# Rotary partners in two tiles: attention for four heads of four key heads at once

## The chip, the cores and the metric

The kernel runs on one core of a Trainium2 chip. The metric is device time in microseconds (us) of one execution of the whole program. Engines are TensorE (PE in the profile, with PEld for its weight loads), VectorE (DVE), ScalarE (ACT), GpSimd (POOL) and SyncE (SP, which here only issues transfers).

## The reference, cut to what matters

The reference is one inference step of a small decoder with two layers on 1024 prompt tokens and eight decode tokens, width 2048. Layer A is a pooling mixer with a gate. After it, keys and values for four key heads of 64 are projected once and shared. Layer B is attention over a window of 128 keys with 32 query heads, eight to a key head, with a sink per head, a gate and an output projection. The first 16 of a head's 64 dimensions are rotated by position ("partial rotary"): dimension i below 8 is the partner of dimension i + 8.

```python
x1, x2, rest = xf[..., :half], xf[..., half:ROT_DIM], xf[..., ROT_DIM:]
out = jnp.concatenate([x1 * cos - x2 * sin, x2 * cos + x1 * sin, rest], axis=-1)
...
s = jnp.einsum('...qkgd,...skd->...kgqs', q, k) * (HEAD_DIM ** -0.5)
p = jnp.exp(s - m);  p = p / (jnp.sum(p, axis=-1, keepdims=True) + jnp.exp(sink - m))
o = jnp.einsum('...kgqs,...skd->...qkgd', p, v);  y = (o * jax.nn.silu(gate)) @ w_out
```

## The kernel before, in words

The prompt is worked in two halves ("chunks"): chunk 0 has 512 tokens, chunk 1 has 512 and the eight decode tokens, 520 columns. Activations lie transposed, channels in partitions and tokens in columns. All large products are made in three passes of split operands: a high part, written by ScalarE (`cast_to`, L488), and a low part, written by VectorE (`prep_to`, L503). Most are made by a Strassen-like scheme of seven half-size products a pair of output tiles (`seven`, L582, products at L658 to L660). Two phases are "plain" (`unit`, L672, products at L686 to L688), and while they run, the sums of weight blocks that the later products need are made by VectorE and stored (`plain_pair`, L293; `first_pair`, L346).

The list `PHASES` sets the order. The attention phases are `bi`: chunk 0, head pairs 0 to 3, plain; chunk 0, pairs 4 to 7, by seven products; chunk 1, pairs 0 to 7, by seven products. After them come the output projections (`bo`). In a plain `bi` phase a unit makes one tile of 128 channels (two heads) by 512 tokens. It has 48 products in four steps of 12. With seven products a pair of tiles takes seven steps of 24 products.

The order of the small work is written by hand against this counter of steps, `self.i`. `at(n, go)` puts work n steps ahead; `product(n, rank, go)` puts PE work at the end of a step, ordered by rank; `posts` are done at the beginning of the next step. `in_order` then fixes the order of the source on PE, VectorE and ScalarE, so a late instruction holds everything behind it on its engine. Loads are issued on SP's queue in program order, a few entries of the weight stream ahead (`ahead`, `load_to`), and each waits until its buffer is free. Buffers are 53 slots of two times 520 columns (`Mem`); a new tile takes the slot that was released longest ago, whole or half.

Attention before the change handles one tile t of 128 query channels at a time: two heads of 64 rows, which belong to two key heads. The order of a head's dimensions is permuted so that the rotary partner of row r is row r + 32 or r - 32. So the rotary step (`q_done`, L1719; `k_done` for keys) copies the tile with neighbouring groups of 32 rows exchanged, by four transfers on SP's queue (`partner`, L1611, issued at L1616), and some steps later (`lag`) multiplies tile and copy by tables of cosine and sine (`rope`, L1624) and adds them (L1731).

`attend` (L1745) then has, for one tile t and all four blocks of 128 tokens: the scores (`score`, L1760), products of a 64-row, 64-column part of PE with 192 keys, into the four PSUM banks of `S`; `select` and `largest` (L1778, L1782, L1786), which put together 8 x 128 scores a row and take the maximum; exponential and sums; `turn` (L1814), eight transposes into the first half of `S`; `keep` (L1823 on ScalarE, L1824 on VectorE), two copies of the transposed weights; the second products (`values`, L1848), in two parts with a GpSimd flag between them (L1856); and `gate` (L1876), which multiplies by the gate and stores. Each has its step: scores at `at`, transposes `s1` steps later, second products `s2` steps after those. So the second products of an earlier tile and the scores of a later one fall on the same step: first part, scores, second part. `gate_done` (L1911) prepares the gate. `t_ops` (L820) makes and stores four differences and sums of a tile, the operands of later seven-product phases.

The next phase's inputs are loaded from `x_begin` on (`x_load`, L759) and split (L769, L778), as slots are free (`x_tick`). The eight decode tokens have their own attention (`dec_keys`, `decode`), for two key heads at a time: once in the middle of the last attention phase and once in the output phase after it, at the steps of `DEC_AT`.

## Time and profile before

| | |
|---|---|
| median of three runs | 2356.75 us (2353.7 to 2358.1) |
| profiled execution, its own time | 2356.38 us |
| span of that execution, first to last instruction | 2354.6 us |
| granted TensorE clock, mean | 0.996 |
| TensorE busy | 2297.3 us, 98% |
| VectorE, ScalarE, GpSimd busy | 82%, 57%, 9% |
| transfers | 665.18 MB, mean 283 GB/s |

A row of a list of groups has the line, engine and operation, then output<-inputs by the program's names, then shape and count; after the bar busy us and mean ns of one; after the next bar the idle time of that engine just before and what ended it. A row of the timeline begins with the start and the duration in us; in brackets is the idle time before it and what ended it. A row of the list of waits reads: who, for whom, us in total, times, longest. In a row of windows each engine has busy us and (in brackets) its instructions, and behind them stand the granted clock, the transfer engines' busy share and GB/s. One matmul of 32-bit operands appears as two instructions, its two passes.

The page's forty slices show how evenly TensorE is filled:

```
PE   8999999999999999999999899999999999999997
DVE  8787998776878878978987788887777768888887
DMA  8668789989889989999786766688777768799785
```

### The profile page before, as it was taken

The numbers are of one execution on the slowest core, as the hardware profiler recorded it, in microseconds if no ns is written. First come the engines' busy times: TensorE is split into PE (matmuls) and PEld (weight loads), VectorE is DVE, ScalarE is ACT, GpSimd is POOL, SyncE is SP. The second block draws the span as 40 slices with busy tenths as digits, with TensorE's granted clock in tenths as the row PEclk, the third lists the DMA queues.
The fourth block names the chain that finished last, engine by engine and source line by source line (L and its number), as shares of the span: only waits on it lengthen the run. The fifth ranks groups of instructions, "written<-read, shape, count | busy, mean of one in ns | idle before, by whom it ended". The sixth has DMA issues, their size and how long they took to land. (4 is left out here: it accounts for less than half of the span.)

```text
span 2354.6 us, 49710 instructions
## 1 busy us (share of the span) xinstructions
PE 2297.3 (98%) x19960; PEld 2200.9 (93%) x19960; DVE 1925.9 (82%) x2421; ACT 1343.1 (57%) x2429; POOL 205.5 (9%) x411
## 2 busy tenths in 40 slices
PE   8999999999999999999999899999999999999997
PEld 6899999999999999998788799999999999999997
DVE  8787998776878878978987788887777768888887
ACT  4444446544546547554465566685666678546556
POOL 0111110001000000000111111100000000000000
PEclk9999999999999999999999999999999999999999
DMA  8668789989889989999786766688777768799785
GB/s 293 211 246 303 271 299 346 332 292 319 289 289 339 327 280 333 328 388 327 272 310 220 248 219 239 224 310 270 237 249 245 230 201 305 239 342 372 260 300 199
DMA packets 250919, 665.18 MB, mean 283 GB/s; under 512 B 25632, under 2 KB 106432, under 8 KB 250688
## 3 DMA queue, kind: packets, MB, share of 16 engines
q1 hardware_dynamic: 205216, 496.94, 63.0%
q0 software_dynamic: 45472, 165.07, 18.1%
q8 instruction: 156, 2.56, 0.4%
q14 instruction: 75, 0.61, 0.1%
HBM read 466.81 MB, written 185.59 MB: 277 GB/s over the span
## 5 line engine op out<-in xcount | busy, mean ns | idle before, releaser
L658 PE MATMUL pD<-m,m 128*128 128x260 f32 (+1 forms) x4752 | 1346.0, 283 | 8.1 <-ACT pD L599 4.4
L660 PE MATMUL pD<-m,m 128*128 128x260 f32 (+1 forms) x4752 | 1339.1, 282 | 4.4 <-DVE m L503 4.4
L659 PE MATMUL pD<-m,m 128*128 128x260 f32 (+1 forms) x4752 | 1338.8, 282 | 0.0
L658 PEld LDWEIGHTS pD<-m,m 128*128 128x128 f32 x4752 | 894.5, 188 | 13.7 <-ACT pD L599 5.5
L660 PEld LDWEIGHTS pD<-m,m 128*128 128x128 f32 x4752 | 895.2, 188 | 5.5 <-DVE m L503 5.5
L503 DVE TENSOR_TENSOR m<-m,m 128x1024 fp32r<-128x1024 f32 x674 | 814.5, 1219 | 100.1 <-ACT m L488 60.6
L659 PEld LDWEIGHTS pD<-m,m 128*128 128x128 f32 x4752 | 894.9, 188 | 0.5
L488 ACT CAST m<-m 128x1024 fp32r<-128x1024 f32 x674 | 702.7, 1049 | 324.7 <-DVE m L346 85.1
L686 PE MATMUL pD<-m,m 128*128 128x512 f32 x448 | 179.7, 401 | 8.0 <-ACT m L769 8.0
L687 PE MATMUL pD<-m,m 128*128 128x512 f32 x448 | 177.9, 397 | 1.0 <-DVE m L778 1.0
L688 PE MATMUL pD<-m,m 128*128 128x512 f32 x448 | 177.5, 396 | 0.0
L778 DVE TENSOR_TENSOR m<-m,m 128x1024 fp32r<-128x1024 f32 (+1 forms) x120 | 147.0, 1226 | 6.4 <-ACT m L769 4.7
L769 ACT CAST m<-m 128x1024 fp32r<-128x1024 f32 (+1 forms) x120 | 125.9, 1053 | 17.7 <-PE pD L687 5.2
L631 ACT COPY m<-pD 128x260 f32<-128x260 f32 (+1 forms) x83 | 31.1, 375 | 179.2 <-PE pD L660 179.1
L346 DVE TENSOR_TENSOR m<-m,m 128x1024 f32<-128x1024 f32 x88 | 107.6, 1222 | 12.7 <-DMA m<-in_wib 6.3
L686 PEld LDWEIGHTS pD<-m,m 128*128 128x128 f32 x448 | 85.1, 190 | 28.1 <-ACT m L769 8.0
L687 PEld LDWEIGHTS pD<-m,m 128*128 128x128 f32 x448 | 85.0, 190 | 21.1 <-DVE m L778 2.1
L688 PEld LDWEIGHTS pD<-m,m 128*128 128x128 f32 x448 | 85.0, 190 | 19.7
L1797 ACT ACTIVATE m<-m,sm 128x128 f32<-128x128 f32 x256 | 99.4, 393 | 0.0
L619 DVE TENSOR_TENSOR m<-pD,m 128x260 f32<-128x260 f32 (+1 forms) x86 | 36.5, 424 | 74.4 <-PE pD L660 74.1
L1088 PE MATMUL pD<-m,m 128*128 128x260 f32 (+1 forms) x528 | 91.5, 323 | 0.0
L1088 PEld LDWEIGHTS pD<-m,m 128*128 128x128 f32 x528 | 79.5, 188 | 8.2
(249 smaller groups left out, 2180.9 us busy)
## 6 DMA issues: line engine op xcount, KB each, us to landing
m<-in_wia SPq DMA_DIRECT2D x124, 512.0 KB
m<-in_wib SPq DMA_DIRECT2D x120, 512.0 KB
swia<-m POOLq DMA_DIRECT2D x64, 512.0 KB, 4.8
m<-swia SPq DMA_DIRECT2D x64, 512.0 KB
m<-swoa SPq DMA_DIRECT2D x64, 512.0 KB
swib<-m POOLq DMA_DIRECT2D x64, 512.0 KB, 5.1
m<-swib SPq DMA_DIRECT2D x64, 512.0 KB
m<-swob SPq DMA_DIRECT2D x56, 512.0 KB
```

The source lines that it names most:

```text
L346: self.nc.vector.tensor_add(s[out].a[:, :1024], s[x].a[:, :1024], s[y].a[:, :1024])
L488: self.nc.scalar.copy(hi.r[:, :1024], self.stream[self.cast].src().a[:, :1024])
L503: self.nc.vector.tensor_sub(lo.r[:, :1024], s.src().a[:, :1024], hi.a[:, :1024])
L658: nc.tensor.matmul(ps[:, :TH], wh[:, s], h, start=new and k == 0, stop=False, skip_group_check=on)
L659: nc.tensor.matmul(ps[:, :TH], wh[:, s], l, start=False, stop=False, skip_group_check=on)
L660: nc.tensor.matmul(ps[:, :TH], wl[:, s], h, start=False, stop=k == 7, skip_group_check=on)
L686: nc.tensor.matmul(ps[:], wh[:, s], h, start=par == 0 and k == 0, stop=False)
L687: nc.tensor.matmul(ps[:], wh[:, s], l, start=False, stop=False)
L688: nc.tensor.matmul(ps[:], wl[:, s], h, start=False, stop=par == 1 and k == 7)
L769: self.nc.scalar.copy(h.r[:, :n], s.a[:, :n])
L778: self.nc.vector.tensor_sub(l.r[:, :n], s.a[:, :n], h.a[:, :n])
L1088: nc.tensor.matmul(ps[:, : cs.stop - cs.start], ws[:, s], d[:, cs], start=f0 and k == 0, stop=l0 and k == 3,)
```

## The change

The heads are reordered: head pair p now stands for four heads, one of each of the four key heads, in two tiles of 128 rows. Tile 0 holds 32 of the dimensions of all four, among them the first rotary half (rows 32g to 32g + 31 for key head g), tile 1 the other 32. Partners are therefore in the same partition of the two tiles, the partner transfers go, and the rotary step is four VectorE operations on the pair. The keys are laid out likewise. A score is then the sum of two products of 32 rows, accumulated in PSUM, and a step of attention takes four heads and half of the blocks (`hf`), where it took two heads and all blocks. Both tiles of a pair must be there before a score.

With it go other edits. In the plain phase the weights come pair after pair, units 0 and 1 of a pair make the queries and 2 and 3 the gates, and both halves of attention hang on one rotary step. Steps are shifted: the rotary step is issued one step after its tiles there, and with lag 2 in place of 3 in the seven-product phases; transposes and second products of the last three halves of the plain phase are one step apart; the gate of the plain phase goes to the next step's beginning; `x_begin` of the plain phase's end comes before the second unit of the last pair. The decode tokens of all four key heads are handled at once, in the output phase. `t_ops` makes two of its differences by one instruction everywhere it is called.

```diff
-DEC_AT = (0, 1, 6, 6, 7, 8, 9, 10, 13, 13), (11, 11, 12, 12, 13, 14, 15, 16, 17, 17)
+DEC_AT = 3, 3, 9, 9, 10, 11, 12, 12, 14, 14
...
-                        q, g = pr("wib", p), pr("wib", 8 + p)
-                        w += q[:2] + g[:2] + q[2:] + g[2:]
+                        w += pr("wib", p) + pr("wib", 8 + p)
...
-        nc.vector.tensor_sub(t[:, 1, :], E[:, a], E[:, b])
-        nc.vector.tensor_sub(t[:, 2, :], E[:, b], O[:, b])
+        E, O = v[:, 0], v[:, 1]
+        h = v.rearrange("p j (h n) -> p j h n", h=2)
+        nc.vector.tensor_sub(t[:, 1:3, :], h[:, 0], h[:, :, 1])
...
-    def partner(self, s, n, T):
-        t = self.mem.full()
-        for a in range(4):
-            b = a ^ 1
-            self.nc.sync.dma_start(t.a[32 * a : 32 * a + 32, : n * T], s.a[32 * b : 32 * b + 32, : n * T])
-        return t
-    def rope(self, s, t, n, T):
-        b2 = lambda x: x[:, None, :].to_broadcast([P, n, T])
-        for a, i in ((s, 0), (t, 1)):
-            v = a.v(n, T)
-            self.nc.vector.tensor_mul(v, v, b2(self.rtab[:, i, :T]))
+    def rope(self, s, T):
+        nc = self.nc
+        u = self.mem.full()
+        v, w = s.v(2, T), u.v(2, T)
+        sin = self.rtab[:, 1, :T]
+        nc.vector.scalar_tensor_tensor(w[:, 0], v[:, 1], -1.0, sin, op0=ALU.mult, op1=ALU.mult)
+        nc.vector.tensor_mul(w[:, 1], v[:, 0], sin)
+        nc.vector.tensor_mul(v, v, self.rtab[:, :1, :T].to_broadcast([P, 2, T]))
+        return u
...
-    def q_done(self, c, t0, s, n, lag):
+    def q_done(self, c, p, s, lag):
...
+        def turn():
+            u = self.rope(s, T)
+            nc.vector.tensor_add(s.a[:, : 2 * T], s.a[:, : 2 * T], u.a[:, : 2 * T])
+            u.free()
...
+        self.at(lag, turn)
...
-            for b in range(NB):
-                for u in (0, 64):
-                    for j in range(2):
-                        r = slice(64 * j, 64 * j + 64)
-                        nc.tensor.matmul(
-                            self.S[u : u + 64, j, b * 256 + u : b * 256 + u + 192],
-                            q[r, b * P + u : b * P + u + 64],
-                            self.kT[t // 8][r, b * P + u : b * P + u + 192], start=True, stop=True,
-                        )
+            for n in range(2):
+                b = 2 * hf + n
+                for i in range(2):
+                    q = s.a[:, i * T : i * T + TP]
+                    for u in (0, 64):
+                        for g in range(4):
+                            r = slice(32 * g, 32 * g + 32)
+                            nc.tensor.matmul(
+                                S4[u : u + 64, g, n * 256 + u : n * 256 + u + 192],
+                                q[r, b * P + u : b * P + u + 64],
+                                self.kT[i][r, b * P + u : b * P + u + 192], start=i == 0, stop=i == 1,
+                            )
...
             if self.i in self.scores:
                 self.product(0, 3, lambda: values(1))
-                self.at(1, gate)
+                if self.strassen:
+                    self.at(1, gate)
+                else:
+                    self.posts.append(gate)
...
-            for t in range(2 * ps[0], 2 * ps[-1] + 2):
...
-                n = t - 2 * ps[-1]
-                self.attend(c, t, 9, *{-1: (11, 1), 0: (13, 2), 1: (8, 2)}.get(n, (14, 2)), n == 0)
-                self.unit(q_done)
-                if t == 2 * ps[-1] - 1:
-                    self.x_begin(nxt)
-                self.last = t == 2 * ps[-1] + 1
-                self.unit(g_done)
+            for p in ps:
+                for hf in range(2):
+                    n = 2 * (p - ps[-1]) + hf
+                    self.attend(
+                        c, p, hf, 10 + 8 * hf, *{-1: (13, 1), 0: (13, 1), 1: (8, 1)}.get(n, (14, 2)), n in (-1, 0)
+                    )
+                box = {}
+                for n in range(4):
+                    def take(ps, n=n, p=p, box=box):
+                        if n % 2 == 0:
+                            box["s"] = self.mem.full()
+                        nc.scalar.copy(box["s"].a[:, n % 2 * T : (n % 2 + 1) * T], ps[:])
+                        if n == 1:
+                            self.q_done(c, p, box["s"], 1)
+                        elif n == 3:
+                            self.gate_done(c, p, box["s"])
+                    if p == ps[-1] and n == 1:
+                        self.x_begin(nxt)
+                    self.last = p == ps[-1] and n == 3
+                    self.unit(take)
...
-            if T > TP and p % 4 == 3:
-                self.at(2, lambda p=p: self.dec_keys(p // 4))
+            if T > TP and p == 7:
+                self.at(6, self.dec_keys)
...
-            self.pair(c, z0, z1, lambda t0=t0, box=box: self.q_done(c, t0, box["s"], 2, 3))
+            self.pair(c, z0, z1, lambda: self.q_done(c, p, box["s"], 2))
...
-                if T > TP and p % 4 == 3:
-                    self.decode(c, p // 4)
+                if T > TP and p == 7:
+                    self.decode(c)
...
-_HEADS = np.array([16 * pr + 8 * j + i for pr in range(2) for i in range(8) for j in range(2)])
+_HEADS = np.array([8 * g + p for p in range(8) for g in range(NKV)])
```

300 lines of the change are left out of this document (143 added, 157 removed).

## The prediction

> **What bounds the kernel now.** I read the page's first part, then the list of what TensorE (PE) waited for, then single waits in the timeline.
>
> ```profile
> span 2354.6 us, 49710 instructions
> PE 2297.3 (98%) x19960; PEld 2200.9 (93%) x19960; DVE 1925.9 (82%) x2421; ACT 1343.1 (57%) x2429; POOL 205.5 (9%) x411
> ```
>
> PE is busy for 98% of the span, so only two things move the end: PE's own work, and the 57 us in which it stands. Another engine matters where it ends one of those waits.
>
> ```profile
> PE pS L1760 <- DVE m L1731: 8.4, 8, 1.5
> PE pD L686 <- ACT m L769: 8.0, 1, 8.0
> PE pO L1848 <- ACT m L1823: 7.8, 1, 7.8
> PE pD L660 <- DVE m L503: 4.4, 5, 1.4
> ...
> PE pS L1760 <- DVE m L1731: 6.8, 6, 1.5
> ```
>
> Columns: us, times, longest. The change can reach two rows: the scores (L1760) waiting for the rotary add (L1731), 8.4 us, and one wait of 7.8 us of the attention's second product (L1848). The 8.0 us are the kernel's first load. The last row is the same view cut to 1345 to 2000 us, the part of the attention phases written with seven products: 6.8 of the 8.4 us lie there, 1.7 us in the first four head pairs of half 0 ("plain" below).
>
> **The rotary partners.** Each rotary step first moves partner rows with four transfers on SP's queue.
>
> ```profile
> L1616 SPq DMA_DIRECT2D m<-m x88: 512/588/2031, 1106.0 to 1957.9; - x88
> ...
>   DMA m<-m: 11.6, 6
> ...
> 1624.94 2.39 DVE L1624 TENSOR_TENSOR m<-m,m 128x1040 f32<-128x1040 f32 x2 [3.86 <-DMA m<-m]
> 1627.37 1.24 DVE L1731 TENSOR_TENSOR m<-m,m 128x1040 f32<-128x1040 f32 x1
> ```
>
> The second row is what VectorE (DVE) idled for ahead of the rotary products (L1624): 11.6 us for the partners. Removed are 88 transfers of 64 KB and 88 x 0.59 = 52 us of SP's time. SP is off PE's path, so that by itself is worth nothing; what counts is the score.
>
> In the seven-product parts the rotary work stays about as long: three operations of 1040 columns before, now two of 520 and two of 1040.
>
> ```profile
> L1624 DVE TENSOR_TENSOR m<-m,m 128x1040 f32<-128x1040 f32 x18 | 21.5, 1236 | 6.8 <-DMA m<-m 6.8
> L1624 DVE TENSOR_TENSOR m<-m,m 128x1024 f32<-128x1024 f32 x10 | 11.8, 1220 | 4.9 <-DMA m<-m 4.9
> L1624 DVE TENSOR_TENSOR m<-m,m 128x512 f32<-128x512 f32 x16 | 10.3, 684 | 0.0
> ```
>
> Before 3 x 1.24 = 3.7 us, after 2 x 0.69 + 2 x 1.24 = 3.9. But it is issued one step earlier (lag 2, not 3; a step there is 24 products of 0.12 us, 2.9 us) and waits for no transfer. The longest wait in this part is 1.5 us, so all six should go: **-6.8 us**, bounds 0 (VectorE late for another reason, such as the buffer of the new temporary) and -6.8.
>
> In the plain part one rotary step now serves two tiles at once, with the same lead as before: two operations of 512 and two of 1024 columns (2 x 0.68 + 2 x 1.22 = 3.8 us) in place of three of 512 (2.05). The first half's score waits for all of it.
>
> ```profile
> 1157.97 1.53 PE L1760 MATMUL pS<-m,m 64*64 64x192 f32 x32 [1.49 <-DVE m L1731]
> ...
> 1203.68 1.23 DVE L1824 TENSOR_TENSOR m<-pS,cst 128x1024 f32<-128x1024 f32 x1 [0.81 <-ACT m L1823]
> 1204.83 1.28 DVE L1624 TENSOR_TENSOR m<-m,m 128x512 f32<-128x512 f32 x2
> 1206.14 0.69 DVE L1731 TENSOR_TENSOR m<-m,m 128x512 f32<-128x512 f32 x1
> ...
> 1207.04 0.28 PE L1848 MATMUL pO<-m,m 64*64 64x128 f32 x2
> 1207.06 0.28 PE L1848 MATMUL pD<-m,m 64*64 64x128 f32 x2
> ...
> 1207.27 0.28 PE L1848 MATMUL pO<-m,m 64*64 64x128 f32 x2
> ...
> 1207.38 0.28 PE L1848 MATMUL pO<-m,m 64*64 64x128 f32 x2
> ...
> 1207.56 0.22 PE L1848 MATMUL pD<-m,m 64*64 64x64 f32 x2
> 1207.60 1.48 PE L1760 MATMUL pS<-m,m 64*64 64x192 f32 x32
> ```
>
> The add ends at 1206.83, 0.77 us before PE is ready. With 1.75 us more it is 1.0 us late. Half as many scores wait: three at 1.0 us, and the first, which waits 1.49 us today (1157.97), about the same; 4.5 less the 1.7 of today is **+2.8 us**. Bounds: -1.7 (VectorE uses the 0.81 us in which it idles ahead) and +4.5 (the first one also grows by 1.75).
>
> **The scores on PE.** A score has 32 products of 64 rows today (16, in two passes), in rounds of four array tiles: 1.48 us less the last one's 0.32, over seven rounds, is 0.16 us a round. The change has 64 products of 32 rows, each as long. Eight tiles at once make again eight rounds of 0.16 us; four at once make sixteen, +1.3 us a score. In the rows above a round of four starts within some 0.02 us (1207.04 and 1207.06, two each), so issue can fill eight tiles in 0.16 us. I take **0**, upper bound 32 x 1.3 = +42.
>
> Then the switch of tile shape. Today scores and second products are both 64x64, and most scores stand between two groups of second products. After the change they are 32x64 between 64x64.
>
> ```profile
> 1209.75 0.23 PE L1848 MATMUL pO<-m,m 64*64 64x64 f32 x2
> 1209.90 0.50 PE L686 MATMUL pD<-m,m 128*128 128x512 f32 x1
> ...
> 1206.88 0.33 PE L1848 MATMUL pO<-m,m 64*64 64x128 f32 x2
> ...
> 1971.46 0.23 PE L1848 MATMUL pD<-m,m 64*64 64x64 f32 x2
> 1971.51 1.48 PE L1760 MATMUL pS<-m,m 64*64 64x192 f32 x32
> ```
>
> Within one shape the next group starts 0.04 us after the last (1207.56 to 1207.60). To another shape it is 0.15 us (1209.75 to 1209.90), 0.11 more, and the first round after a switch takes 0.16 us (1206.88 to 1207.04) where a later one takes 0.11 (1207.27 to 1207.38), 0.05 more: 0.16 us a switch. 24 of the 32 scores stand so, the first at 1207.60, the last at 1971.51; two new switches each are 48 x 0.16 = **+7.7 us**. No row has a switch between 64 and 32 rows; the bounds are 0 (only the tile changes) and 7.7. I take the nearest row that changes shape.
>
> The Trainium skill speaks against the change here: "TensorEngine Tiling (Array Packing)", Key Properties, says that a change of tiling mode, not of the tile alone, drains the array, and its list has 64x64 and 32x64 as different modes. By it the 7.7 us are paid, without it they are 0. The trace agrees for 64x64 to 128x128; for 64 to 32 rows no row here shows it.
>
> The same skill's "TensorE: Matmul & The Clock Gate", Wait — 56ns, not 53.3ns?, puts a floor of about 25 ns between starts. By it a score would need 64 x 25 = 1.6 us, not 1.3, some 10 us over 32 (an estimate from that page). The trace differs: two rows of "x2" start within 0.01 to 0.02 us.
>
> **The stall of 7.8 us.** At the end of the plain part a weight load came late.
>
> ```profile
> 1259.18 0.98 SPq L759 DMA_DIRECT2D m<-h  x2
> ...
> 1267.93 0.36 SPq L759 DMA_DIRECT2D m<-th  x1
> ...
> 1320.73 0.99 SPq L287 DMA_DIRECT2D m<-in_wib  x1
> ...
> 1328.94 1.22 DVE L346 TENSOR_TENSOR m<-m,m 128x1024 f32<-128x1024 f32 x1 [5.75 <-DMA m<-in_wib]
> 1330.20 1.04 ACT L488 CAST m<-m 128x1024 fp32r<-128x1024 f32 x1 [9.02 <-DVE m L346]
> 1333.73 1.00 ACT L1823 COPY m<-pS 128x1024 f32<-128x1024 f32 x1
> 1334.79 0.48 PE L1848 MATMUL pO<-m,m 64*64 64x128 f32 x2 [7.79 <-ACT m L1823]
> 1336.87 0.32 PE L1848 MATMUL pD<-m,m 64*64 64x64 f32 x2
> 1337.11 0.79 PE L686 MATMUL pD<-m,m 128*128 128x512 f32 x1
> 1340.66 0.39 PE L688 MATMUL pD<-m,m 128*128 128x512 f32 x1
> 1312.00:1345.00 33.00, 24.65 (x239) 19.47 (x231) 24.33 (x31) 13.29 (x31) 5.84 (x13) 0.84 0.89 282
> ```
>
> The load issued at 1320.7 held up VectorE's sum (L346), the cast behind it on ScalarE (ACT), the copy of the transposed scores queued behind that, and PE. The clock fell too (0.84 over these 33 us): the group at 1334.79 took 2.08 us where the same group at 1206.88 took 0.68, and the nine starts to 1340.66 took 3.55 us where 9 x 0.23 = 2.1 is usual. In all 7.8 + 1.4 + 1.45 = 10.7 us.
>
> Three edits touch it. The partner transfers leave SP's queue. The plain weights are loaded pair after pair instead of two pairs interleaved, so two raw tiles of each pair are held for about four steps less. Against that, the loads of the next part's inputs (L759) may begin only before the third last unit, where now it is before the fifth last; a unit is 48 products of 0.23 us, 11 us. I take half, **-5.3 us**, from bounds of -10.7 (gone) and +9.3 (second rival).
>
> **The rest, at 0.** The fused difference in the Strassen helper saves an instruction of some 0.15 us on VectorE each time; PE is not held by it, and were VectorE the bound it would be a gain. The decode tokens' attention, two steps today (one in the middle of the last attention phase, one in the output phase), becomes one step in the output phase: its score takes 128 passes instead of twice 32, in four tiles instead of two, and one more cache load, eight more one-row transfers and a longer use of the score banks fall into that phase. Its own steps run one or two apart, covered by 2.9 us of products each; with that cover gone they would cost 1 or 2 us. Gate, softmax and stores keep their size; a store has half as long rows, off the path. The normalised scores' copy has one step instead of two at two more places (bound +1).
>
> **The sum.** -6.8 + 2.8 + 7.7 - 5.3 = -1.6 us on the profiled execution's 2356.38 us (0.4 us under the median of the runs shown, 2356.75): **2354.8 us**, with its own range 2347 to 2361. A measurement of this kernel tells a difference from about 0.2%, 4.7 us; so no change that can be told.
>
> **Rivals.**
> First, no drain between 64 and 32 rows: the 7.7 us fall away, 2347.1, and with the stall wholly gone 2341.8. For it: a change of tile within a shape costs 0.04 us. Against it: every change of shape in the trace costs more.
> Second, slower: the next part's input loads crowd the end of the plain part. Five loads of 512 KB issued today from 1259 to 1268 us move behind 1300; 2.6 MB at the 282 GB/s of the row above are 9.3 us, and the transfer engines are 89% busy there already. If they do not fit, the weights come 9.3 us later still and the stall becomes 10.7 + 9.3: 2354.8 + 5.3 + 9.3 = 2369. It decides once more than the free 11% of those 33 us, 3.6 us of transfers, is moved there. Against it: SP's queue stood idle for buffers before 1312, which the shorter holding eases.
> Third, the eight tiles do not run at once: +42, 2397. Against it are the rounds above.
>
> **Chances.** Forecast 0.50 (faster 0.18, same 0.30, slower 0.02), first rival 0.25 (faster), second 0.19 (same 0.01, slower 0.18), third 0.06 (slower). Together faster 0.43, same 0.31, slower 0.26. The range goes from the first rival's 2342 to just under the second's full price, 2368; what is left out is the third and the edges.
>
> **What would show it.** Right: no row of partner transfers; the score no longer waiting for the rotary add after 1345, and waiting about 1 us at three places before; 64 products a score in about 1.5 us; 0.15 us instead of 0.04 from second product to score; the wait of L1848 below 7.8 us. Wrong: 0.04 us at those switches (first rival), a longer wait near 1330 (second), a score of 2.6 us (third), or new waits of the decode step in the output phase.

## The result and the profile after

The changed kernel takes 2369.9 us (median of six runs, 2363.96 to 2372.57) where the kernel before took 2354.77 beside it (six runs, 2353.63 to 2358.1): a ratio of 1.0060, 95% interval 1.0046 to 1.0073. By that ratio it is 14 us slower. The forecast was 2354.8 us, no change that can be told, with a range up to 2368. The profiled execution, 2363.96 us, happens to be the fastest of the six, so some waits in it may be shorter than they usually are; a second profile stands below (e1).

Further down, a ratio to the kernel before is turned into us by multiplying what it differs from 1 (or from another ratio) by 2354.77.

The first part of the page after, and its list of what TensorE waited for (us, times, longest):

```profile
span 2362.1 us, 51581 instructions
...
PE 2308.3 (98%) x21048; PEld 2207.6 (93%) x21048; DVE 1928.6 (82%) x2356; ACT 1339.9 (57%) x2424; POOL 203.3 (9%) x395
```

```profile
...
PE pS L1831 <- DVE m L1807: 6.7, 4, 5.5
PE pD L657 <- DVE m L618: 6.5, 6, 2.4
PE pO L659 <- DVE m L502: 5.0, 1, 5.0
...
PE pD L1831 <- POOL flag L1840: 2.4, 4, 0.9
```

No score (L1743) waits for VectorE any more: the 8.4 us are gone, also the 1.7 of the plain part. The 7.8-us wait at the plain end has become one of 5.5 (second products behind the masked copy, L1807). And there is a new kind of wait, 5.0 us of the output product L659 for the rounding of its weights (L502). Before, the same product (one line higher in the source) waited for it only this long:

```profile
PE pO L660 <- DVE m L503: 0.2, 1, 0.2
```

Where the time went is seen by laying the two traces over each other: the start of the n-th product of the seven-product helper (lines 657 to 659) in each trace less its start in the kernel before. The first two columns lie in the plain phase, and there it is the n-th product of the plain helper (lines 685 to 687). The numbers are us of difference; the last stretch reaches to the last such product.

```
before, at         1162  1324  1424  1512  1771  1818  1951  1995  2042  2082  2153   end
after             -0.9  -0.9  +0.5  +2.0  -1.5  -4.4  -4.1  +0.4  +6.7  +7.2  +7.4  +7.5
after, again (e1) +0.3  +0.3  +1.7  +4.7  +1.2  -1.7  -1.5  +3.9 +16.4 +18.1 +17.7 +18.2
e5                +0.9  +1.0  +4.8  +8.4  +5.1  +2.2  +2.5  +7.0 +13.0 +11.9 +12.4 +11.5
e13               -0.6  -0.5  +3.3  +6.0  +2.8  -0.1  +0.1  +4.9  +5.7  +6.7 +14.7 +12.6
e17               +0.6  +0.7  +4.8  +6.1  +2.4  -0.6  -0.3  +4.2  +8.9  +8.6  +8.8  +8.9
```

The last three rows belong to experiments below. At 1951 us the changed kernel is ahead, by 4.1 us in the first profile and 1.5 in the second. 2.9 of that lead (1771 to 1818) are only the first decode step, which it does later. Then, where the last attention phase goes over into the output phase, it loses 11 us within 91 (1951 to 2042), in the second profile 18. That is the place that the prediction had put at nothing. The rows of the timeline there (start, duration, line; in brackets the idle time before and what ended it):

```profile
2021.72 0.75 DVE L1869 SCALAR_TENSOR_TENSOR m<-pS,m 128x256 f32<-128x256 f32 x2
2022.87 0.72 POOL L1874 DMA_DIRECT2D o<-m  x1 [8.04 <-DVE m L1869]
...
2025.62 1.23 DVE L502 TENSOR_TENSOR m<-m,m 128x1024 fp32r<-128x1024 f32 x1 [3.16 <-DMA o<-m]
2026.88 1.04 ACT L487 CAST m<-m 128x1024 fp32r<-128x1024 f32 x1 [8.17 <-DVE m L502]
...
2026.90 0.58 PE L659 MATMUL pO<-m,m 128*128 128x256 f32 x1 [5.00 <-DVE m L502]
```

VectorE gates the last head group (L1869), GpSimd stores the result (L1874), and VectorE's next work, the rounding of output weights, stands until that store has landed; it starts 2.75 us after the store's issue. ScalarE's cast and TensorE stand behind it. Ten traces here have this wait (this one, e1, e2 and e5 to e11). In all ten the semaphore that the rounding waits for is that of the store, and the rounding starts 0.19 us after the store's last part has landed. The landing takes 2.6 us from the issue in three of them (this one, e2, e5) and 5.0 to 6.9 us in the other seven.

The tile shapes, in one score with its neighbours on TensorE:

```profile
1869.73 0.23 PE L1831 MATMUL pO<-m,m 64*64 64x64 f32 x2
1869.74 0.23 PE L1831 MATMUL pD<-m,m 64*64 64x64 f32 x2
1869.90 1.56 PE L1743 MATMUL pS<-m,m 32*64 32x192 f32 x64
1871.38 0.33 PE L1831 MATMUL pD<-m,m 64*64 64x128 f32 x2
...
1871.54 0.28 PE L1831 MATMUL pD<-m,m 64*64 64x128 f32 x2
...
1871.77 0.28 PE L1831 MATMUL pD<-m,m 64*64 64x128 f32 x2
...
1871.88 0.28 PE L1831 MATMUL pD<-m,m 64*64 64x128 f32 x2
```

64 passes take about the 1.5 us that 32 took, so eight tiles do run at once. Into the score it is 0.16 us where it was 0.04, and the first round of second products behind it takes 0.16 where a later one takes 0.11 (1871.77 to 1871.88). Over the 24 scores that stand between second products, it is 1.63 us from the last of these to the first one behind the score, where it was 1.34 (medians of the two traces).

And the plain end:

```profile
1330.94 2.48 DVE L346 TENSOR_TENSOR m<-m,m 128x1024 f32<-128x1024 f32 x2
...
1333.51 1.06 ACT L487 CAST m<-m 128x1024 fp32r<-128x1024 f32 x1 [4.29 <-DVE m L346]
...
1338.52 0.99 ACT L1806 COPY m<-pS 128x1024 f32<-128x1024 f32 x1
1339.54 1.22 DVE L1807 TENSOR_TENSOR m<-pS,cst 128x1024 f32<-128x1024 f32 x1 [3.00 <-ACT m L1806]
...
1340.82 0.92 PE L1831 MATMUL pS<-m,m 64*64 64x128 f32 x16 [5.52 <-DVE m L1807]
```

VectorE's sum of weights (L346) waits for no load now, but comes after other work of VectorE. ScalarE's cast stands 4.3 us for it, and the copy of the transposed scores (L1806) is behind that cast on ScalarE. Some 20 us later stands a second wait that the kernel before doesn't have there: 2.4 us of L657 for VectorE's sum (L618), up to 1362.5 us.

### The profile page after: what moved, and what is told of

The parts are those of the page before. It is cut to its first block, busy times and chain, and to the rows that moved or that the text cites. A ratio compares the mean times of both kernels' runs of the same rounds, so it can differ in the third digit from the quotient of the medians.

```text
span 2362.1 us, 51581 instructions
## 1 busy us (share of the span) xinstructions
PE 2308.3 (98%) x21048; PEld 2207.6 (93%) x21048; DVE 1928.6 (82%) x2356; ACT 1339.9 (57%) x2424; POOL 203.3 (9%) x395
## 5 line engine op out<-in xcount | busy, mean ns | idle before, releaser
L657 PE MATMUL pD<-m,m 128*128 128x260 f32 (+1 forms) x4752 | 1347.9, 284 | 11.5 <-DVE m L618 6.5
L659 PE MATMUL pD<-m,m 128*128 128x260 f32 (+1 forms) x4752 | 1340.7, 282 | 4.8 <-DVE m L502 4.6
L657 PEld LDWEIGHTS pD<-m,m 128*128 128x128 f32 x4752 | 896.0, 189 | 17.9 <-ACT pD L598 6.4
L659 PEld LDWEIGHTS pD<-m,m 128*128 128x128 f32 x4752 | 896.4, 189 | 6.5 <-DVE m L502 6.5
L502 DVE TENSOR_TENSOR m<-m,m 128x1024 fp32r<-128x1024 f32 x674 | 813.9, 1219 | 85.4 <-ACT m L487 57.4
L346 DVE TENSOR_TENSOR m<-m,m 128x1024 f32<-128x1024 f32 x88 | 107.6, 1222 | 10.9 <-DMA m<-in_wib 5.1
L618 DVE TENSOR_TENSOR m<-pD,m 128x260 f32<-128x260 f32 (+1 forms) x86 | 36.5, 424 | 84.3 <-PE pD L659 84.0
```

Source lines behind the costliest of these rows:

```text
L346: self.nc.vector.tensor_add(s[out].a[:, :1024], s[x].a[:, :1024], s[y].a[:, :1024])
L502: self.nc.vector.tensor_sub(lo.r[:, :1024], s.src().a[:, :1024], hi.a[:, :1024])
L657: nc.tensor.matmul(ps[:, :TH], wh[:, s], h, start=new and k == 0, stop=False, skip_group_check=on)
L659: nc.tensor.matmul(ps[:, :TH], wl[:, s], h, start=False, stop=k == 7, skip_group_check=on)
```

## The experiments

**e1, the changed kernel again, unaltered.**

> The changed kernel, unaltered, for a second profile: its median is 6 us above the execution profiled first (2363.96 us). Theory A (the change into the output phase): the extra 6 us lie between the last attention phase and the output phase, 1950 to 2050 us, as a longer wait and a longer stretch of lower clock; time 2369 to 2372 us. Theory B (the switches of tile shape around each score): the loss is spread evenly over the scores, and this profile differs from the first one nowhere in particular.

2374.49 us in one run. The waits of TensorE and VectorE between 1985 and 2060 us:

```profile
PE pO L659 <- DVE m L502: 9.2, 1, 9.2
...
DVE m L502 <- DMA o<-m: 7.3, 1, 7.3
```

The same place, nearly twice as long. What differs between the two profiles is how long the store takes to land (2.6 and 6.7 us), and how long the clock stays low behind the wait (3.4 and 10.2 us).

**e2, the gathered decode score in two runs of 64 passes, steps 2 and 3, in place of 128 passes at step 3.** The first run lies in score banks that the prompt still uses, so the prompt's output is not the reference's.

```
-        def s0():
-            for b in range(NDEC):
+        def s0(b0=4):
+            for b in range(b0, b0 + 4):
...
+        self.product(2, 1, lambda: s0(0))
```

> The decode tokens' score, 128 passes in one run of 3.7 us, is divided in two runs of 64, one step apart. Theory A: the granted clock no longer falls behind it (0.66 at 1995 to 2000 us in the first profile), and the kernel gains 2 us against the changed kernel in a quiet execution, up to 8 in a usual one: 2362 to 2368 us. Theory B: no gain, 2369 to 2371 us.

2367.05 us, ratio 1.0050 (1.0035 to 1.0065). Stretches of the changed kernel and of e2 (busy time of each engine, the last three numbers are granted clock, DMA share and GB/s):

```profile
1992.00:1996.00 4.00, 4.00 (x125) 3.98 (x123) 0.68 (x2) 3.03 (x6) 0.00 (x0) 0.98 1.00 340
1996.00:2000.00 4.00, 4.00 (x36) 3.87 (x42) 4.00 (x4) 0.15 (x1) 0.00 (x0) 0.60 0.54 188
```

```profile
1996.00:2000.00 4.00, 4.00 (x64) 3.85 (x62) 1.89 (x3) 1.94 (x5) 0.72 (x1) 1.00 0.86 287
2000.00:2004.00 4.00, 4.00 (x73) 3.98 (x71) 2.57 (x3) 2.94 (x6) 0.00 (x0) 1.00 0.91 322
```

Behind the 3.75 us of the gathered score (1991.5 to 1995.2 us) TensorE's clock falls to half for 3.4 us, though TensorE was busy all along. Behind two runs of 1.9 us it doesn't, here and in e16. That is worth 1.7 us; the intervals of the two times don't separate it. The wait for L502 stays.

The length of the run isn't all. Of the 14 traces with the score in one run, 13 have the fall, and that of e5 doesn't: its run, from 1998.1 to 2001.9 us, is as long, and the clock stays up behind it.

```profile
2000.00:2005.00 5.00, 5.00 (x100) 4.84 (x107) 3.04 (x4) 1.70 (x5) 0.00 (x0) 1.00 0.88 303
2005.00:2010.00 5.00, 5.00 (x94) 4.72 (x95) 5.00 (x5) 3.74 (x6) 0.00 (x0) 1.00 0.40 128
```

In each of the 20 traces the stretches of low clock start whole multiples of 3.413 us apart, and all but the last one last a whole multiple of it. So the clock is set window by window, and it matters where a run lies. In e5 the next boundary (2000.2 us) cuts the run into 2.0 and 1.5 us of products; in e17 the larger piece has 1.8 us, and the clock falls all the same, so the place in the window doesn't explain every case.

**e3 and e4, the changed kernel and the kernel before, each without its decode step** (the decode tokens' attention and cache updates are left out).

```
-                    self.decode(c)
+                    self.at(14, lambda: [
+                        nc.sync.dma_start(self.act["o", c][:, i::2, TP:], self.sgd[:, i]) for i in range(2)
+                    ])
```

> The changed kernel without the attention of the decode tokens: the gate alone is stored in its place, and the updated key and value caches of the decode tokens are not written. Theory A: what the change loses goes with it, 2345 to 2350 us, no slower than the kernel before with the same left out. Theory B: it keeps its loss of 8 to 15 us over that kernel, 2355 to 2363 us.

> The kernel before with the same left out (decode tokens' attention and their cache updates). Both theories: its PE work of 2 x 2.8 us and some switches go, 2346 to 2350 us; it is the measure for the run without decode attention of the changed kernel.

e3: 2352.42 us, ratio 0.9983 (0.9973 to 0.9992). e4: 2343.88 us, ratio 0.9954 (0.9939 to 0.9969). So the decode step costs 1.0060 - 0.9983, 18.1 us, in the changed kernel and 10.8 before: 7.3 of the 14.1 us are the decode step (to about 5 us, by the intervals), and 6.8 are the rest of the change (to about 4). In e3 the long wait is gone; all that TensorE waits for between 1985 and 2090 us is

```profile
PE pD L659 <- DVE m L502: 2.2, 2, 1.4
PE pS L1831 <- DVE m L1807: 0.8, 1, 0.8
```

Two causes, then, one in each half. They aren't quite apart: in the kernel before, about half of what the scores wait for the rotary add goes with the decode step. Its row has 8.4 us before and in e4

```profile
PE pS L1760 <- DVE m L1731: 4.3, 5, 1.5
```

The change removes these waits in any case. So beside them the gathered decode step loses about 7.3 + 4.1 = 11.4 us, and not 7.3 (an estimate, from one trace of each kernel).

**e7, the scores as 32 passes of 64 rows in place of 64 of 32 rows**, all else as in the changed kernel. Each product stands alone in its bank; in the changed kernel two are summed.

```
-                        for g in range(4):
-                            r = slice(32 * g, 32 * g + 32)
+                        for g in range(2):
+                            r = slice(64 * g, 64 * g + 64)
...
-                                self.kT[i][r, b * P + u : b * P + u + 192], start=i == 0, stop=i == 1,
+                                self.kT[i][r, b * P + u : b * P + u + 192], start=True, stop=True,
```

> The changed kernel with the scores as 32 products of 64 rows in four array tiles, as in the kernel before, in place of 64 products of 32 rows. Each product then sums over the rows of two heads, so the scores are not the reference's; all other work is the same in number, size and order. Theory 'tile shapes': 24 of 32 scores cost 0.34 us less, -8.3 us, 2361 to 2362. Rival: TensorE makes up for the switches in its waits elsewhere: less than 2 us, 2368 to 2370.

2364.1 us, ratio 1.0031 (1.0021 to 1.0041): 6.8 us less, with intervals that are apart. From the second products ahead of a score to those behind it is 1.34 us again. This is the tile shapes' price, although this run's profile had a long wait for L502 (8.6 us). e14, below, gives 7.3 us for the same edit on another base.

**e5, the stored tile marked as late for longer** (`self.mem.release(a, 60 if p == 7 else 10)` in place of `a.free(True)`).

> The changed kernel with one edit: the tile in which the last head group's gated values are stored counts as busy for 60 further allocations (10 before), so that nothing is written into its slot while the store is under way. Nothing is left out. Theory 'store': the 5.0 us for which TensorE stands for VectorE's rounding of the first output weights (line 502, late for a transfer out of the tile it writes) goes, and with it the half-clock time behind it, 1.7 us: 2362 to 2364 us, 0.997 to 0.9975 of the changed kernel. Theory 'weights': the transfer that is late is a load of weights that stands behind the 16 one-row transfers on SP's queue; then the wait stays, and the time is 2369 to 2370. Rival 'tile shapes': the wait may go, but the time moves by less than 2 us, since most of the loss is in the switches.

2368.55 us, ratio 1.0051 (1.0038 to 1.0064). The wait is still there, still for the store:

```profile
2028.02 0.72 POOL L1874 DMA_DIRECT2D o<-m  x1 [8.05 <-DVE m L1869]
2030.76 1.23 DVE L502 TENSOR_TENSOR m<-m,m 128x1024 fp32r<-128x1024 f32 x1 [3.15 <-DMA o<-m]
```

The kernel's own bookkeeping says why. Counting through `Mem` (L135), one of the 53 tiles is free when the rounding asks for its tile: the one that the gate released in the same step. A mark of lateness only orders the free tiles, and with one free there is nothing to order. In the kernel before there are at least two free at each step of this stretch, and none that is taken has a store under way.

**e6, the next part's inputs at the plain end loaded two units earlier; e8, the transposes of the two late steps there one step earlier.**

```
-                    if p == ps[-1] and n == 1:
+                    if p == ps[-1] - 1 and n == 3:
                         self.x_begin(nxt)
```

```
-        *{-1: (13, 1), 0: (13, 1), 1: (8, 1)}.get(n, (14, 2)), n in (-1, 0)
+        *{-1: (12, 2), 0: (12, 2), 1: (8, 1)}.get(n, (14, 2)), n in (-1, 0)
```

> The changed kernel with the loads of the next part's inputs at the plain end begun before the fifth last unit again, as in the kernel before, not before the third last. Nothing is left out. Theory 'inputs': at 1326 to 1340 us VectorE's three subtractions (line 777, 1.22 us each) and ScalarE's two casts (line 768, 1.03 us each) of these inputs stand ahead of the weights' sums and of the softmax, and make the 5.5 us for which TensorE waits for the masked copy (line 1807): with them two units earlier the wait goes, -5.5 us and -1.7 us of half clock, 2363. Rival: the inputs only fill time; the wait stems from the one step that the copy has lost (turn and copy in one step), and stays: 2368 to 2371.

> The changed kernel with the transposes of the two 'late' attention steps at the plain end one step earlier, so that a step lies between turn and copy and another between copy and products, as in the kernel before (steps 12 and 2 in place of 13 and 1). Nothing is left out. Rival of e6_x_early: the 5.5 us wait for the masked copy is the lost step; then it goes, 2363. Theory 'inputs': the normalised probabilities come late at 1336 us, because ScalarE stands 4.3 us for VectorE's sum of weights; then the transposes wait instead of the products, and the time stays within 3 us of 2369.9.

e6: 2370.61 us, ratio 1.0059 (1.0046 to 1.0071), no change. e8: 2375.06 us, ratio 1.0076 (1.0063 to 1.0089). The waits of e6 and, below, of e8:

```profile
PE pO L659 <- DVE m L502: 8.4, 1, 8.4
...
PE pS L1831 <- DVE m L1807: 5.7, 3, 4.7
```

```profile
PE pD L659 <- DVE m L502: 11.6, 4, 6.0
...
PE pO L659 <- DVE m L502: 7.4, 1, 7.4
...
PE pS L1831 <- DVE m L1807: 4.1, 3, 3.0
```

At the plain end the wait of 5.5 us falls to 4.7 and to 3.0. By the starts of the products both edits win more than that: from 1324 to 1424 us e6 and e8 take 0.5 and 0.6 us less than the kernel before, where the changed kernel takes 1.4 to 1.5 more (the table). So the loads' place has a part in the loss and the lost step too. What was won there was lost again at 2030 us, and in e8 in a further wait of 6.0 us up to 2143. Neither could be judged before the wait in the output phase was understood.

**e9, the decode tokens' value rows by way of memory, without the 16 one-row transfers; e12, the same edit in the kernel before; e10, e9 with e7's scores.**

```
-                for b in range(NDEC):
-                    nc.sync.dma_start(
-                        dv[P - 1 : P, b, :], self.vd[P - NDEC + b : P - NDEC + b + 1, i * P : (i + 1) * P]
-                    )
...
+                nc.sync.dma_start(dv[: P - 1], io["cv"][i, : P - 1])
+                nc.sync.dma_start(dv[P - 1 :], io["nvs"][i, P - 1 :])
...
-                nc.sync.dma_start(io["nvs"][i], dv)
+                nc.sync.dma_start(io["nvs"][i, : P - 1], dv[: P - 1])
...
```

> The changed kernel in which the decode tokens' rows of the value cache no longer go by 16 one-row transfers on SP's queue at the start of the output phase. They are written to the new cache in memory once, right after they are computed at the start of half 1 (two transfers), and each cache load reads its last row from there; the store of the cache follows two steps later. Nothing is left out. Theory 'queue': at 2014 to 2031 us the 16 transfers take 13.5 us of SP's queue, partly behind the cache loads that they wait for, and the output weights' loads (line 287) stand between and behind them; these come late, and VectorE's rounding (line 502), the cast and TensorE after it. Then the wait of 5.0 to 8.6 us at 2027 to 2035 us goes, with 1.7 to 3.4 us of half clock: 7 to 12 us less than the 2369.9 of the changed kernel, 2358 to 2363, a ratio to the kernel before of 1.001 to 1.003. Rival 'store': the wait is for a store of gated values out of the slot that is written next; then the wait stays, and the time is within 2 us of 2369.9.

> e9_rows_early and the scores of e7_rows64 together (32 products of 64 rows, whose sums run over two heads and are not the reference's scores). If the one-row transfers and the tile shapes are the two causes and independent, their effects add: 7 to 12 and 6.8 us less than the changed kernel, 2351 to 2356, a ratio of 0.998 to 1.000. If TensorE only exchanges one wait for another, less than 10 us in all, 2360 or more.

> The kernel before with the edit of e9_rows_early: no one-row transfers in its two decode steps. Theory 'queue' for the changed kernel alone: the kernel before has 8 such transfers at a time, in two places, and no wait of over 2 us for an output weight, so at most 2 us less, ratio 0.999 to 1.000. Rival: the one-row transfers cost each kernel about the same, and gathering them isn't what made the change slower; then 5 us less or more, ratio below 0.998.

e9: 2431.29 us (ratio 1.0311, 1.0294 to 1.0329), e10: 2425.0 (1.0284, 1.0265 to 1.0302) and e12: 2413.17 (1.0235, 1.0216 to 1.0254): by the ratios 55 to 60 us slower than the kernels they start from (the changed one, e7 and the one before), which none of the theories had foreseen. The edit loads and stores 127 partitions where it was 128. From 2035 to 2080 us of e9 the transfer engines are almost idle (tenths of 16 engines in 40 slices, then GB/s), and VectorE's sum of weights (L346) waits 62.0 us for output weights, whose loads stand on SP's queue among these transfers:

```profile
DMA  0000010000000000000000000000940000000000
GB/s 25 25 25 25 25 40 25 29 25 25 25 25 25 25 25 25 25 25 25 29 25 25 25 25 29 25 25 25 313 178 25 25 25 29 25 25 25 29 25 25
```

25 GB/s where whole tiles move at ten times that. The Trainium skill states the rule ("DMA: Bandwidth & Descriptors", Why a DMA increments its semaphore by 16 and not by 1): the number of engines is the largest up to 16 that divides the slowest dimension, and 127 partitions get one. The trace agrees: from 2047 to 2065 us the busy share of the 16 engines is 0.06, one of 16. So the times of e9, e10 and e12 say nothing of the one-row transfers. One reading is left in e9: with no such transfer on SP's queue, VectorE still stood for the store.

```profile
2026.21 0.72 POOL L1876 DMA_DIRECT2D o<-m  x1 [8.05 <-DVE m L1871]
...
2032.12 1.23 DVE L502 TENSOR_TENSOR m<-m,m 128x1024 fp32r<-128x1024 f32 x1 [6.31 <-DMA o<-m]
```

**e11, the decode scores in 32 products of 64 rows** (the same edit as in e7, in `s0`).

> The changed kernel with the decode tokens' scores in 32 products of 64 rows in place of 64 products of 32 rows; each sums over the rows of two heads, so the decode scores are not the reference's. All else as in the changed kernel. Theory 'low clock': the run of small products at 1991 us (3.75 us, 8 columns each) lowers TensorE's clock for 3.4 to 6.8 us behind it; at half the length (1.9 us) the run costs 1.9 us less and the clock stays up, another 1.7 us: 2366. Rival: the run is long because of its weight loads, 128 of them, which stay 64 at least, and the clock falls for another reason: 2368 to 2370.

2369.43 us, ratio 1.0043 (1.0030 to 1.0057), not told apart from the changed kernel. Its score in the trace (count, duration in ns, first and last start):

```profile
L1961 PE MATMUL pS<-qd,m x64: 252/253/273, 1995.6 to 1999.1; 64*128 64x8 f32 x64
```

Those of the changed kernel and of one of the two decode steps of the kernel before (count, busy us, mean ns):

```profile
L1961 PE MATMUL pS<-qd,m 32*128 32x8 f32 x128 | 3.8, 252 | 0.0
```

```profile
L1964 PE MATMUL pS<-qd,m 64*128 64x8 f32 x32 | 2.0, 254 | 0.0
```

Half the passes take the same 3.75 us, and the clock falls behind them as before. The kernel before spends 2.0 us twice. So the gathered score isn't longer; it is only in one piece.

**e13, the value caches taken two steps later, and with them their one-row transfers and the decode values; e14, e13 with e7's scores.**

```
-DEC_AT = 3, 3, 9, 9, 10, 11, 12, 12, 14, 14
+DEC_AT = 3, 3, 9, 9, 10, 11, 12, 12, 16, 16
...
-        self.at(8, v0)
-        self.at(10, v1)
+        self.at(10, v0)
+        self.at(12, v1)
```

> The changed kernel with the two decode value caches taken and loaded two steps later (steps 10 and 12 in place of 8 and 10) and the decode values two steps later (16 in place of 14). Nothing is left out; the 16 one-row transfers stay on SP's queue. Theory 'slots': the gathered decode step holds two more tiles and a longer work tile of the 53 in the pool; at step 9 one tile is left, that of a store just begun, and VectorE's rounding (line 502) gets it. With the caches later it gets another, and the wait of 5.0 to 9.3 us with 1.7 to 5 us of half clock goes: 7 to 12 us less than the changed kernel, ratio 1.001 to 1.003. Rival 'queue': the weights' loads behind the one-row transfers are what is late; then a wait of the same length appears two steps later, ratio 1.005 to 1.006.

> e13_v_later with the scores of e7_rows64 (32 products of 64 rows, sums over two heads, not the reference's scores). If slots and tile shapes are the two causes, their effects add: 7 to 12 and 6.8 us less than the changed kernel, ratio 0.998 to 1.000. If either only shifts a wait, 1.002 or more.

e13: 2369.59 us, ratio 1.0055 (1.0041 to 1.0069). e14: 2363.09 us, ratio 1.0024 (1.0015 to 1.0033). The time of e13 is the changed kernel's, but its trace settles the question at 2030 us. With two tiles more at that moment the rounding starts before the store is even issued:

```profile
2026.62 1.22 DVE L502 TENSOR_TENSOR m<-m,m 128x1024 fp32r<-128x1024 f32 x1
2027.12 0.72 POOL L1874 DMA_DIRECT2D o<-m  x1 [8.05 <-DVE m L1869]
...
2030.51 1.88 SPq L1944 DMA_DIRECT2D m<-m  x3
```

The stretch that cost 6.3 us (12.5 in e1) costs 0.8. The one-row transfers (L1944) are all there, two steps later with the caches, and no such wait follows them (TensorE's longest is 1.7 us until 2090). It was the tile, not the queue. The gain went at 2137 us:

```profile
PE pD L659 <- DVE m L502: 5.9, 1, 5.9
```

This is all that TensorE waits for between 2100 and 2150 us. It follows a late load of the attention's output (VectorE's difference of it, L827, stood 6.0 us for it), and the edit had also moved the decode step's end by two steps. But e8, which moves nothing of the decode step, has the same wait of 6.0 us at the same product, behind the same late load (6.1 us), so the later end isn't needed for it.

**e17, e13 with the decode values at step 15 in place of 16; e18 and e19, e17 with the edits of e6 and e8.**

> The changed kernel with the value caches two steps later (10 and 12 in place of 8 and 10) and the decode values one step later (15 in place of 14; e13: 16). Nothing is left out. If the new wait at 2137 us of e13 is from the later end of the decode step, which shifts the order in which tiles come free, it goes, and the gain of the transition stays: 6 to 9 us less than the changed kernel, ratio 1.002 to 1.0035. If the shortage of slots only moves from place to place, 1.005 to 1.006 again.

> e17_v_later15 with the next part's inputs at the plain end loaded two units earlier, as in e6. Nothing is left out. If e6's gain at the plain end was real and only lost again at the transition: 2 to 4 us less than e17, ratio 1.001 to 1.002. If it was chance: as e17.

> e17_v_later15 with the transposes of the two late attention steps at the plain end one step earlier, as in e8. Nothing is left out. e8's trace gained 2 to 4 us at 1424 us and lost 16 us at the transition and behind it. If the loss was the slots': 2 to 4 us less than e17, ratio 1.001 to 1.002. If the waits of the output phase come in any case: 1.004 or more.

e17: 2365.3 us, ratio 1.0035 (1.0021 to 1.0049). The wait at 2137 us is gone and that at 2030 stays away; between 1985 and 2160 us there is left

```profile
PE pD L659 <- DVE m L502: 3.0, 3, 1.6
PE pO L659 <- DVE m L502: 1.7, 1, 1.7
PE pS L1831 <- DVE m L1807: 0.7, 1, 0.7
PE pD L657 <- ACT pD L598: 0.4, 1, 0.4
```

That is 5.9 us less than the changed kernel by the ratios, whose intervals just overlap. Not all of the transition is won: e17 still loses 4.7 us from 1995 to 2042 us where e13 loses 0.8, with the same wait of 1.7 us, because the clock falls behind it in the one run and not in the other (e13, then e17):

```profile
2025.00:2030.00 5.00, 3.26 (x28) 3.05 (x27) 5.00 (x8) 3.09 (x10) 0.72 (x1) 1.00 0.81 240
```

```profile
2025.00:2030.00 5.00, 3.26 (x19) 3.06 (x18) 5.00 (x9) 3.09 (x11) 0.72 (x1) 0.76 0.71 237
```

By the windows of e2 this is chance: in e17 the wait (2025.7 to 2027.4 us) lies whole in one of them (2024.2 to 2027.6), in e13 a boundary at 2026.4 cuts it, as boundaries do in e18 and e19, where the clock stays up too.

e18: 2362.88 us, ratio 1.0026 (1.0015 to 1.0036). e19: 2360.4 us, ratio 1.0016 (1.0006 to 1.0027), 10.4 us less than the changed kernel, with intervals that are apart. e18 is 2.1 us below e17 and e19 4.5, by medians whose intervals overlap; on their own the edit of e6 had changed nothing and that of e8 had cost 3.8, with intervals that overlap too. e19 is the best kernel here with the change; it is still slower than the kernel before.

**e16, the whole decode step later, its score in two runs** (score at steps 12 and 13, value caches at 14, values at 19). Its scores lie in banks in which the prompt's last second products are still summed, so the prompt's output isn't the reference's.

> The changed kernel with the whole gathered decode step later: key caches loaded at step 9, scores in two runs of 64 passes at steps 12 and 13 (128 at step 3 in the changed kernel), the work tile taken with the scores, value caches at 14, values at 19, and the next part's differences at 20 in place of 18. Nothing is left out. By the slots and the clock together: no wait for line 502 at 2027 to 2035 us, no half clock behind the scores: 8 to 14 us less than the changed kernel, ratio 1.000 to 1.0025. If the decode work only carries its waits to the later steps, ratio 1.004 to 1.006.

2362.52 us, ratio 1.0018 (1.0009 to 1.0027): 9.9 us less, with intervals that are apart. At 1995 to 2050 us neither the wait nor the low clock is left; a wait of 4.0 us near 2059 has come in with the later values, for VectorE's sum (L618).

## Why the prediction was wrong

The step that failed is "the rest, at 0", in its part on the decode step: "covered by 2.9 us of products each; with that cover gone they would cost 1 or 2 us". It costs 7.3 us more than before (e3, e4). I had counted the gathered step's work, passes, loads, transfers and banks, and not what it holds of the one pool from which every engine takes its tiles. When the rounding asks for its tile, it holds two value tiles and a whole work tile (the two key tiles have been given back), where the kernel before held a key tile and half a work tile, and there was not one to spare. With one tile free, VectorE's rounding got the one whose store had just begun, and a store that was off everyone's path came to set TensorE's pace: it lands 2.6 us after its issue in the quick profile and up to 6.9 in others, and the low clock comes behind it. e13 shows the cause in the trace. Its size is less sure: 5.9 us by the medians of e17, whose interval touches the changed kernel's, and 9.9, with intervals apart, when the whole step is moved and its score divided (e16). On top comes the low clock behind the gathered score (1.7 us in 13 of 14 traces). Of what would make it wrong, the prediction's last words came true: new waits of the decode step in the output phase.

The second failure is the plain end. "I take half, -5.3": it cost 1.4 and 1.5 us more than before in the two profiles of the changed kernel (1324 to 1424 us) and 1.3 in e16's, but 3.7 to 4.3 in seven others with the same code there (e2, e3, e5, e9, e11, e13, e17). The seven have one more stretch of low clock, behind the wait of 2.4 us for L618: 2.2 us or more of it lie in one window of the clock, and at most 1.7 in the other three. So the changed kernel's own two profiles were lucky there. The late load was gone, as the edits promised, but its place was taken: VectorE was late with the sum, ScalarE with the copy behind it. The second rival had the moved loads as the mechanism, by weights that come later still. That isn't what happened, since the sum of weights waits for no load, and that its price, 2369 us, is within 1 us of the measured time is luck. But the moved loads have a part: with them moved back the wait is 4.7 us in place of 5.5 (e6), and the stretch to 1424 us 3.3 us shorter (e18 against e17); by what way is not shown. The edit put at "0, bound +1", one step less for the copy at two more places, has one too: with the step given back the wait is 3.0 us (e8), the stretch 4.8 us shorter and the time 4.5 us less (e19 against e17; the intervals of these times overlap, so this size is likely rather than shown).

The drain between tile shapes was right in place and size: 7.7 us forecast, 6.8 (e7) and 7.3 (e14 against e13) measured. The first rival, no drain, is out. A switch between 64 and 32 rows costs what one between 64 and 128 does. The Trainium skill's rule ("TensorEngine Tiling (Array Packing)", Key Properties), by which a change of mode drains the array, holds here: 0.16 us into the score against 0.04, in the rows above.

Eight tiles at once, at 0, was right (third rival out). The scores' waits, -6.8, went as forecast. In the plain part the other bound was the true one: not +2.8 but -1.7, since no score waits there either. The bound's reason was wrong, though. VectorE idles more there, 5.2 us where it was 0.81 ahead of the masked copy. But ScalarE is free when the transposes end, and its copy starts 0.3 us behind them and not 1.5, so the masked copy and the rotary step behind it are 1.2 us earlier; the add ends 0.2 to 0.3 us before three of these scores. A slip touches no sum: of the 88 partner transfers 32 have 64 KB, the others 128 or 130.

The range ended at 2368 with the second rival's price. No rival had the decode step, and none a shortage of tiles. With what the runs showed the terms are -6.8 for the scores' waits, -1.7 in the plain part, 6.8 to 7.3 for the tile shapes, 1.3 to 4.3 at the plain end and, by the estimate of e3 and e4, 11.4 for the decode step: 11 to 14.5 us, where the ratio says 14.1.

What stays open: why the load behind the later wait of 6 us comes late in e8, e13 and e14 and not in the others, and how the remaining 3.8 us of e19 divide. It pays about 7 for the tile shapes, so the rest of the change now gains some 3 (an estimate).

## What to carry to other kernels

When work is gathered into one step, count what it holds and for how long, not only what it issues: in a pool that runs down to its last tile, one tile more ties an engine to a store that nobody waited for. Read a wait on "DMA, a store" ahead of an operation that reads nothing from it as a question of whose tile is written. And judge a small edit only when the large wait behind it is gone: by the medians the same one-step edit cost 3.8 us ahead of it and won 4.5 without it, though neither size is clear of the noise.

## What the runs showed of the hardware

- Loads and stores of 127 partitions ran at 25 GB/s and cost three kernels 55 to 60 us (e9, e10, e12), a far larger effect than anything that was being tested.
- TensorE's clock fell to half for 3.4 us or more behind 3.75 us of products of 8 columns, with TensorE busy throughout, in 13 of 14 traces, and not behind two runs of 1.9 us (e2, e16). So it isn't only a wait that lowers it.
- In all 20 traces stretches of low clock begin whole multiples of 3.413 us apart. In ten traces with the same code there, a wait of 2.4 us near 1362 us lowered the clock seven times, when 2.2 us or more of it lay between two such boundaries, and not in the three with at most 1.7 (e3 and e1, for example).
- 64 passes of 64 rows and 128 passes of 32 rows of those 8-column products take the same 3.75 us (e11); the passes of the further tiles are free.
- One program varied from 2363.96 to 2374.49 us. Its two profiles differ by 8 us at one place (1951 to 2082 us): a store that took 6.7 us to land and not 2.6, and the low clock behind the wait for it. The same wait of 1.7 us lowered the clock in one program and not in the next (e17, e13).
